# The first stage and the attention heads of a diffusion-transformer step, written out by hand for four queues

## Chip, cores and metric

The kernel runs as one program on one core of a Trainium2 chip. The metric is the time of one execution on the device in microseconds (us). The matmul engine TensorE is called PE in the profile, VectorE is DVE, ScalarE is ACT, GpSimd is POOL, and SyncE, whose queue issues nearly all DMAs here, is SP.

## The reference

Two streams of 256 tokens with 1024 features (the image tokens `x` and the context `ctx`) pass two layers. Each layer is: a SwiGLU feed-forward, a mixer, a second feed-forward; each part is preceded by an RMS norm that is modulated by a shift and a scale, and added back through a gate. Shift, scale and gate are columns of `silu(c) @ mod_w[i] + mod_b[i]`, one set for each stream. The mixer of layer 0 is a gated short convolution, that of layer 1 is attention with 8 query heads of 128 features and 2 key/value heads, whose keys are both streams (512) and whose queries are the image tokens (256).

```
for i in range(2):
    mod  = (silu(c) @ mod_w[i] + mod_b[i]).reshape(3, 3, D)        # shift, scale, gate, three times
    modc = (silu(c_ctx) @ mod_w[i] + mod_b[i]).reshape(3, 3, D)
    lat = lat + 0.5 * mod[0, 2] * swiglu(rms(lat) * g * (1 + mod[0, 1]) + mod[0, 0], w13, w2)   # and ctx
    lat = lat + mod[1, 2] * mixer(...)                              # conv, then attention
    lat = lat + 0.5 * mod[2, 2] * swiglu(..., w13', w2')
# attention, for each head: p = softmax(q k^T / sqrt(128)), p v, then @ w_o
```

Everything is float32. Layer 1 needs the context for its keys and values alone, so its last feed-forward runs on the image tokens only.

## The kernel before

**Layout.** Activations lie features on partitions, tokens along the free axis: `x` is 8 tiles of 128 features by 512 tokens (256 of each stream). A float32 product is made of three matmuls in a rounded format (`mm3`, lines 124 to 126 of the profile): each operand is split into a rounded high part and the rest (`split`: ACT copies to the high part, line 100, DVE subtracts, line 101), and the products high-high, high-low and low-high are summed in PSUM. So every weight that comes from memory into a `wr` tile (three of them, 1 MB each, `load_raw`, line 96, on SP) passes through ACT and DVE before PE can use it (`wh`, `wl`, four 1024-wide pairs). `hop` is a pool of sixteen 1024-wide operand tiles (`hot`), PSUM has six 512-wide tiles in one ring (`psum`) and two in another (`psmall`).

**Modulation.** The first two groups of modulation columns, shift B00 and scale A00 of the first norm, are made by PE in the first stage (`mod_pe`, steps P: eight small matmuls; `mod_turn`, steps T, turns the rows into columns; DVE adds the bias). All others are made on DVE, beside PE's work: a unit (`mod_unit`, line 154, `junk`) is a 1024-wide product and sum against the broadcast `silu(c)`, and a weight load of 1 MB in a `wr` tile serves two to four units. `tick(n)` puts n units at a place of the program.

**Order.** A scheduler orders each engine's instructions by its own estimates and priorities, except in the first stage, where PE's order alone is written out by hand (`FIRST_STEPS` inside `manual_schedule`). There, N is a quarter of the norm (DVE makes t = x*A*r, ACT hh = t + B, DVE hl), H the float32 copy of it that later sums need, W a block's weight load with its splits, M a quarter of a block's products, F fillers that keep PE busy, S the broadcast of `silu(c)`. The first three of 22 blocks of the first feed-forward are made in this stage: 144 matmuls of 512 columns. Behind it come `h.sums()`, the sums and splits of the norm's output that later blocks use (a Strassen-like scheme, class `Pair`), and `tick(4)`.

**DMA order.** SP's loads, and the ten small constants that ACT's queue loads (`cload`), take completion semaphores in turn from eight; a DMA waits until the one eight places ahead of it has landed, whichever queue that was issued from.

**Attention.** `scores(hd)` makes, for each of two query tiles, the 128 x 512 scores on PE (`psc`), their maximum (`mx`) and `nb` on DVE, the exponential `e` with its sum on ACT, the reciprocal `r` on DVE and the normalized `pn` on POOL. `turn` transposes `pn` on PE (`pt`) and splits it (`pth`, `ptl`); `mix` multiplies by the values on PE (`pav`) and splits the result (`a`). The program names them head by head, two heads ahead, and the scheduler orders all engines. The output projection (`py`) follows; its weights `wo` are four loads, split whenever the scheduler places it.

**Last feed-forward.** Image tokens only; the first four blocks run on operands that don't yet need the norm's sum (`Early`), the rest on both halves side by side (`mm_wide`, lines 132 and 134). Three modulation loads of the last gate fall into it and use `wr` tiles.

Of the kernel before, what the change touches and what calls it, by code (L numbers as in the profile page):

```python
# [16 lines left out]
P = 128  # L17
# [13 lines left out]
WARM = 36  # L31
FILL = 8
# [5 lines left out]
    "P10 P00 T10 T00 N0 F W0 M00 W1 P11 P01 T11 T01 N1 H0 M10 W2 M01 P12 H1 M11 P02 T12 T02 "  # L38
    "N2 M20 H2 M21 P13 P03 T13 T03 N3 M02 M12 M22 H3 M03 M13 M23 S"
# [4 lines left out]
def hybrid_kernel(ctx: ExitStack, tc: tile.TileContext, a: dict, out: bass.AP):  # L44
# [40 lines left out]

    sccol = const.tile([P, KT, 32], F32, name="sccol", tag="sccol")
# [12 lines left out]
    def split(hi, lo, src):  # L99
        nc.scalar.activation(out=hi, in_=src, func=AF.Copy)  # L100
        nc.vector.tensor_tensor(out=lo, in0=src, in1=hi.bitcast(F32), op=ALU.subtract)  # L101
# [45 lines left out]

    def mod_unit(l, ch, pair, raw, j, v):
# [5 lines left out]
        nc.vector.tensor_tensor_reduce(  # L154
            out=junk,
            in0=raw[:, j * D : j * D + D],
            in1=scbc[:, v, :],
            scale=1.0,
            scalar=modb[:, l, col : col + 1],
            op0=ALU.mult,  # L160
            op1=ALU.add,
            accum_out=mt[:, kt, v : v + 1],
        )
        done[l, ch] += 1
# [4 lines left out]
    def mod_job(l, ch, pair):  # L169
        mod_tile(l, ch)  # L170
        raw = load_raw(a["modT"][l, ch * 4 + pair])
# [9 lines left out]
    def next_unit():  # L181
        if not units:
            l, ch, pair = jobs.pop(0)
            mod_tile(l, ch)
            raw = load_raw(a["modT"][l, ch * 4 + pair])
# [544 lines left out]
    def ffn(l, b, h, tot, gate, tail, gs=(), ev=1.5, z=None):  # L730
        gs = list(gs)
        i0 = 0
        for t, n in enumerate(THIRDS):
            between = ()
            if tot == T2:
# [22 lines left out]
                for i in range(len(gs), n):  # L758
                    if t == 0 and not heads and i in AS_IS[l, b]:
                        w = load_w(a["w13"][l, b, i])  # L760
                        pp = psum("pg"), psum("pu")
                        if prev:
                            prev.seven()
                        w13_mm(pp, w, h, range(4), 0, T2)
# [109 lines left out]

    def mod_pe(ch, q):


        raws = []
        for i in range(2):
            raws.append(hot("pm", F32))  # L880
            nc.sync.dma_start(raws[i], a["mod0"][ch, q, :, i * 1024 : i * 1024 + 1024])
# [28 lines left out]
    def norm_q(q):  # L910
        k2 = slice(2 * q, 2 * q + 2)
        nc.vector.tensor_tensor(
            out=A00[:, k2, :], in0=A00[:, k2, :], in1=both(normg[:, 0, 0, k2]), op=ALU.mult
        )
        for k in range(2 * q, 2 * q + 2):
            for s in range(2):
                t = None
                if k % 2:
                    t = tp.tile([P, T2], F32, name=nm("t"), tag="sg", bufs=3)[:, :S]
                ts[k, s] = norm_k(s, k, h, A00, B00, ris[s], t)  # L920

    def copy_q(q):
        for s in range(2):
            h32[q, s] = gp.tile([P, T2], F32, name=nm("hr"), tag="gl" if s else "gh")
            for k in range(2 * q, 2 * q + 2):
                nc.scalar.activation(
                    out=h32[q, s][:, (k % 2) * S : (k % 2) * S + S], in_=ts[k, s],
                    func=AF.Identity, bias=B00[:, k, s : s + 1],
                )

    pps = {}
    ris, ts = [], {}

    def first_mm(i, q):
        if q == 0:
            pps[i] = psum("pg"), psum("pu")
        w13_mm(pps[i], ws[i], h, range(2 * q, 2 * q + 2), 0, T2)

    ws, gs0 = {}, []

    def load_sc():
        for v in range(2):
            nc.sync.dma_start(scbc[:, v, :], a["c2"][v : v + 1, :].to_broadcast([P, D]))
            nc.scalar.activation(out=scbc[:, v, :], in_=scbc[:, v, :], func=AF.Silu)

    def first_w(i):
        if i < 2:
            ws[i] = load_w(a["w13"][0, 0, i], fine=True)
            return
        raw = load_raw(a["w13"][0, 0, i])  # L950
        parts = [new_pair("w") for _ in range(4)]
        for j in (0, 2, 1, 3):
            split(*parts[j], raw[:, j * T2 : j * T2 + T2])
        ws[i] = lambda o: tuple(t[:, o % T2 : o % T2 + P] for t in parts[o // T2])
# [5 lines left out]
        "H": copy_q,  # L960
        "S": load_sc,
        "W": first_w,
        "N": norm_q,
        "M": first_mm,
    }
    with tc.manual_schedule(engines={mybir.EngineType.PE}):
        fill(WARM)
        sums = [rms_sum(s, (accs[s], accs[s, "last"])) for s in range(2)]
        for step in FIRST_STEPS.split():
            if step == "P00":  # L970
                for s in range(2):
                    ris.append(tp.tile([P, S], F32, name=nm("ris"), tag=f"ris{s}", bufs=1))
                    nc.scalar.copy(ris[s], rms_all(*sums[s]))
# [6 lines left out]
    h.sums()  # L980
    tick(4)

    convk = cload("convk", [P, 3, KT])
    qg = cload("qg", [P, 1])
    kg = cload("kg", [P, 1])
    cosT = cload("cosT", [P, S])
    sinT = cload("sinT", [P, S])
# [3 lines left out]
    ffn(0, 0, h, T2, lazy_gate(0, 0), tail_norm(0, 1, hn), gs0, 1.8)  # L991
# [42 lines left out]
    def by_pairs(key):  # L1034
        box = {}
# [21 lines left out]
    ffn(1, 0, h, T2, lazy_gate(1, 0), tail_norm(1, 1, hn), (), 1.4)  # L1057
# [134 lines left out]
    def scores(hd):  # L1192
        kv = hd // (HEADS // KVH)
        r_ = []
        for qt in range(2):
            o = (hd % 2) * S + qt * P
            ps = psum("psc")
            mm3(ps, tuple(t[:, o : o + P] for t in qs[hd // 2]), ks[kv], True, True)
            ci = hd * 2 + qt
            mx = ap.tile([P, 1], F32, name=nm("mx"), tag="mx", bufs=4)  # L1200
            nc.vector.reduce_max(mx, ps, axis=AX.X)
            nb = ap.tile([P, 1], F32, name=nm("nb"), tag="nb", bufs=4)
# [4 lines left out]
            e = tp.tile([P, T2], F32, name=nm("e"), tag="sg", bufs=3)  # L1207
            sm = ap.tile([P, 1], F32, name=nm("sm"), tag="smx", bufs=4)
            nc.scalar.activation(
                out=e, in_=ps, func=AF.Exp, scale=scq[:, ci : ci + 1], bias=nb, accum_out=sm  # L1210
            )
            r = ap.tile([P, 1], F32, name=nm("r"), tag="r", bufs=4)
            nc.vector.reciprocal(r, sm)
            if qt == 0:
                pn2 = hot("pn", F32)
            pn = pn2[:, qt * T2 : qt * T2 + T2]
            nc.gpsimd.tensor_scalar(out=pn, in0=e, scalar1=r, scalar2=None, op0=ALU.mult)
            r_.append(pn)
        return r_

    def turn(pn):
        pth, ptl = (hot(t).rearrange("p (b q) -> p b q", q=S) for t in ("pth", "ptl"))
        for qt in range(2):
            pt = psum("pt")
            for kt in range(4):
                nc.tensor.transpose(
                    pt[:, kt * P : kt * P + P], pn[qt][:, kt * P : kt * P + P], ident
                )
            split(
                pth[:, :, qt * P : qt * P + P], ptl[:, :, qt * P : qt * P + P],  # L1230
                pt.rearrange("p (k q) -> p k q", k=4),
            )
        return pth, ptl

    aos, at = [], []

    def mix(hd, pt):
        kv = hd // (HEADS // KVH)
        if hd % 2 == 0:
            t = hot("a")  # L1240
            at.append((t[:, :T2], t[:, T2:]))
        po = psum("pav")
        for kt in range(4):
            vw = tuple(t[:, kv * P : kv * P + P] for t in vs[kt])
            mm3(po[:, :S], vw, (pt[0][:, kt, :], pt[1][:, kt, :]), kt == 0, kt == 3)
        o = (hd % 2) * S
        ah, al = (t[:, o : o + S] for t in at[-1])
        split(ah, al, po[:, :S])
        aos.append((ah, al))

    pns, pts = {0: scores(0)}, {}
    v_proj(2)
    v_proj(3)
    tick(2)
    pns[1] = scores(1)
# [10 lines left out]
    project(  # L1266
        by_pairs("wo"), lambda k, c0, c1: aos[k], KT, lazy_gate(1, 1), tail_early(1, 2, hn, hz), S, 0, 0,
# [85 lines left out]
```

## Time and profile before

| | us |
|---|---|
| median of 3 runs (lowest, highest) | 1580.02 (1578.83, 1580.3) |
| the profiled execution | 1575.39 |
| its span on the core | 1573.6 |
| mean granted TensorE clock | 0.998 |
| PE busy | 1556.6 (99%) |
| DVE busy | 1330.8 (85%) |
| ACT busy | 735.2 (47%) |
| DMA, mean over the span | 158 GB/s |

The profiled execution's own time is 1.8 us above its span. Starts are counted from the start of the span. A matmul's duration is modelled and longer than its place in the pipeline: two wide matmuls that follow each other start about 0.23 us apart, though each is listed with 0.39. In brackets behind an instruction stands the idle time of its engine ahead of it and what ended that.

### The profile page before, as it was taken

The page shows a single profiled execution, that of the slowest core. Times are in us where ns is not written, and L with a number is a line of the kernel's source. Part 1 is how long each engine was busy: PE and PEld are TensorE (multiplying, and loading weights), DVE is VectorE, ACT ScalarE, POOL GpSimd, SP SyncE. Part 2 cuts the span into 40 slices and gives each one's busy share as a digit, 9 for nine tenths or more (in the row PEclk, how much of TensorE's full clock was granted, in tenths as well). Part 3 has the DMA queues.
Part 4 walks back from the last instruction along what each step waited for, and adds up shares of the span by engine and source line. Part 5 has one row for each costly group of instructions (what it writes and reads, how often), then busy time and mean ns, then how long its engine had stood idle before and what let it go on. Part 6 is the DMA issues. An engine that isn't in the chain of part 4 may idle for free.

```text
span 1573.6 us, 25030 instructions
## 1 busy us (share of the span) xinstructions
PE 1556.6 (99%) x10224; PEld 1421.7 (90%) x10224; DVE 1330.8 (85%) x2065; ACT 735.2 (47%) x1164; POOL 26.1 (2%) x20
## 2 busy tenths in 40 slices
PE   9999999999999999999999999999999999999999
PEld 7788998999888899989999899999899898898888
DVE  5989789979988779898798899788798889797676
ACT  6522452544322355435345375335345355665553
POOL 0000000000000000000000000000000003300000
PEclk9999999999999999999999999999999999999999
DMA  9565245334554422452353423442453555256552
GB/s 363 201 223 184 90 146 179 114 128 155 185 200 175 161 68 101 159 184 86 129 176 110 167 84 113 158 158 101 155 187 125 212 180 174 80 201 229 177 208 97
DMA packets 39571, 248.74 MB, mean 158 GB/s; under 512 B 5408, under 2 KB 7200, under 8 KB 14624
## 3 DMA queue, kind: packets, MB, share of 16 engines
q1 hardware_dynamic: 36864, 245.38, 43.8%
q10 hardware_dynamic: 2592, 1.76, 0.4%
q8 instruction: 80, 1.31, 0.3%
q14 instruction: 35, 0.29, 0.1%
HBM read 244.77 MB, written 1.05 MB: 156 GB/s over the span
## 4 chain that ended last, share of the span: by engine, by line
PE 93%; DVE 3%; ACT 2%; DMA 2%; issue 0%; ACTq 0%; DVEq 0%
PE py L125 9%; PE py L126 9%; PE py L124 9%; PE p L126 7%; PE p L125 7%; PE p L124 7%; PE q L124 5%; PE q L126 5%; PE q L125 5%; PE py L132 2%; PE pg L132 2%; PE pu L132 2%; PE pu L126 1%; PE pg L124 1%; PE pu L125 1%; PE pu L124 1%
## 5 line engine op out<-in xcount | busy, mean ns | idle before, releaser
L100 ACT ACTIVATE wh<-wr 128x1024 fp32r<-128x1024 f32 (+2 forms) x276 | 276.4, 1014 | 350.0 <-PE py L125 107.1
L101 DVE TENSOR_TENSOR wl<-wr,wh 128x1024 fp32r<-128x1024 f32 (+2 forms) x276 | 320.7, 1168 | 57.1 <-ACT wh L100 56.8
L154 DVE CUSTOM_DVE_ANT_0 junk<-wr,scbc,modb 128x1024 bf16<-128x1024 f32 x224 | 287.2, 1282 | 32.5 <-DMA wr<-in_modT 30.0
L124 PE MATMUL py<-gh,wh 128*128 128x512 f32 (+1 forms) x570 | 213.3, 374 | 0.0
L125 PE MATMUL py<-gl,wh 128*128 128x512 f32 (+1 forms) x570 | 213.2, 374 | 0.0
L126 PE MATMUL py<-gh,wl 128*128 128x512 f32 (+1 forms) x570 | 213.0, 374 | 0.0
L101 DVE TENSOR_TENSOR wl<-ws,wh 128x1024 fp32r<-128x1024 f32 x108 | 131.8, 1223 | 26.2 <-ACT wh L100 25.9
L100 ACT ACTIVATE wh<-ws 128x1024 fp32r<-128x1024 f32 x108 | 113.7, 1058 | 80.2 <-PE p L125 32.8
L126 PEld LDWEIGHTS py<-gh,wl 128*128 128x128 f32 x570 | 107.3, 188 | 19.0
L124 PEld LDWEIGHTS py<-gh,wh 128*128 128x128 f32 x570 | 107.4, 188 | 18.6
L125 PEld LDWEIGHTS py<-gl,wh 128*128 128x128 f32 x570 | 107.4, 188 | 18.2
L126 PE MATMUL p<-th,wl 128*128 128x256 f32 x432 | 122.3, 283 | 0.0
L125 PE MATMUL p<-tl,wh 128*128 128x256 f32 x432 | 122.2, 283 | 0.0
L124 PE MATMUL p<-th,wh 128*128 128x256 f32 x432 | 122.2, 283 | 0.0
L534 DVE SCALAR_TENSOR_TENSOR x<-py,G,x 128x256 f32<-128x256 f32 x189 | 83.9, 479 | 25.1 <-PE py L126 12.1
L124 PE MATMUL q<-bh,wh 128*128 128x256 f32 x320 | 90.6, 283 | 0.0
L125 PE MATMUL q<-bl,wh 128*128 128x256 f32 x320 | 90.6, 283 | 0.0
L126 PE MATMUL q<-bh,wl 128*128 128x256 f32 x320 | 90.6, 283 | 0.0
L124 PEld LDWEIGHTS p<-th,wh 128*128 128x128 f32 x432 | 82.9, 192 | 0.3
L125 PEld LDWEIGHTS p<-tl,wh 128*128 128x128 f32 x432 | 82.9, 192 | 0.3
L126 PEld LDWEIGHTS p<-th,wl 128*128 128x128 f32 x432 | 82.9, 192 | 0.0
L676 DVE TENSOR_TENSOR ws<-wr 128x1024 f32<-128x1024 f32 x54 | 65.8, 1219 | 0.7 <-DMA wr<-in_w 0.7
(288 smaller groups left out, 4019.3 us busy)
## 6 DMA issues: line engine op xcount, KB each, us to landing
wr<-in_w SPq DMA_DIRECT2D x88, 1024.0 KB, 4.9
wr<-in_modT SPq DMA_DIRECT2D x64, 1024.0 KB, 4.9
wr<-in_w2b SPq DMA_DIRECT2D x32, 896.0 KB, 4.6
wr<-in_w2a SPq DMA_DIRECT2D x16, 1024.0 KB, 4.8
pm<-in_mod SPq DMA_DIRECT2D x16, 512.0 KB, 9.2
wr<-in_cw_cx SPq DMA_DIRECT2D x8, 1024.0 KB, 4.9
wr<-in_cw_b SPq DMA_DIRECT2D x4, 1024.0 KB, 5.8
wr<-in_cw_out SPq DMA_DIRECT2D x4, 1024.0 KB, 4.9
```

The source lines that it names most:

```text
L100: nc.scalar.activation(out=hi, in_=src, func=AF.Copy)
L101: nc.vector.tensor_tensor(out=lo, in0=src, in1=hi.bitcast(F32), op=ALU.subtract)
L124: nc.tensor.matmul(ps, wh, mh, start=first, stop=False, **kw)
L125: nc.tensor.matmul(ps, wh, ml, start=False, stop=False, **kw)
L126: nc.tensor.matmul(ps, wl, mh, start=False, stop=last, **kw)
L132: nc.tensor.matmul(ps, w[0], m[2], start=first and n == 0, stop=False)
L154: nc.vector.tensor_tensor_reduce(out=junk, in0=raw[:, j * D : j * D + D], in1=scbc[:, v, :], scale=1.0, scalar=modb[:, l, col : col + 1], ...
L534: nc.vector.scalar_tensor_tensor(out=x[:, m, s * S : s * S + S], in0=ps[:, o : o + S], scalar=g[:, m, s : s + 1], in1=x[:, m, s * S : s * ...
L676: tt(out=sm.rearrange("p (a b c) -> p a b c", a=2, b=2)[:, :, 0, :], in0=a21.unsqueeze(1).to_broadcast([P, 2, T2]), in1=self.raw[:, T2 : 3 ...
```

## The change

- **First stage, all four queues.** The order of PE, DVE, ACT and SP is written out. Loads are steps of their own (L a modulation load; R half of a block's weights, two 512-wide quarters, 0.5 MB), W splits a single quarter, X makes the inverse norms, U makes x*g*r ahead of the modulation, N does one 128-feature tile (ACT hh from A and B, the float32 copy in place on DVE or ACT, DVE hl). The first products of blocks 0 and 1 are named by part: h is high-high, w uses the low part of the weights, l that of the activations. Fillers: 32 and 5 instead of 36 and 8. A Silu on a constant stands ahead of the first real one. The constants for the convolution and the attention are issued behind the stage's last Silu; `h.sums()` moves into block 3's code, `tick(4)` is gone, and two feed-forwards have larger ticks.
- **Attention.** The order of PE, DVE, ACT and POOL is written out over all heads, with the last two `v_proj` between the first two heads. The first two loads of `wo` come ahead of the heads, and each is split in four quarters, one in each of loop steps 2 to 5 and two in each of the last two; where there is a head to run ahead, the quarter stands ahead of its second exponential. The `tick(2)` between the heads is gone.
- **Last feed-forward.** From the output projection on, a modulation load goes as two halves into operand tiles of `hop` and no longer into a `wr` tile.

```diff
-WARM = 36
-FILL = 8
+WARM = 32
+FILL = 5
 FIRST_STEPS = (
-    "P10 P00 T10 T00 N0 F W0 M00 W1 P11 P01 T11 T01 N1 H0 M10 W2 M01 P12 H1 M11 P02 T12 T02 "
-    "N2 M20 H2 M21 P13 P03 T13 T03 N3 M02 M12 M22 H3 M03 M13 M23 S"
+    "L10 L00 R00 R10 P10 X U0 L11 P00 L01 T10 T00 W00 N00 W01 N01 F h000 w000 l000 R20 W10 "
+    "W11 h001 w001 h100 h101 l001 l100 l101 U1 P11 L12 P01 L02 T11 T01 w100 w101 N10 N11 W20 "
+    "W21 U2 M01 R01 R11 P12 L13 P02 L03 T12 T02 M11 R21 N20 N21 W02 W03 M20 W12 W13 U3 M21 "
+    "P13 P03 T13 T03 W22 W23 M02 N30 N31 M12 M22 M03 M13 M23 S"
 )
...
+    def load_mod(l, ch, pair):
+        src = a["modT"][l, ch * 4 + pair]
+        if not roomy:
+            raw = load_raw(src)
+            return raw[:, :D], raw[:, D:]
+        raw = hot("wm", F32), hot("wm", F32)
+        for j in range(2):
+            nc.sync.dma_start(raw[j], src[:, j * D : j * D + D])
+        return raw
...
+    def scale_q(q):
...
+                nc.vector.scalar_tensor_tensor(
+                    out=raw_of(k, s), in0=x[:, k, s * S : s * S + S],
+                    scalar=normg[:, 0, 0, k : k + 1], in1=ris[s], op0=ALU.mult, op1=ALU.mult,
+                )
+    def norm_one(q, j):
...
+            nc.scalar.activation(
+                out=hs[s][0], in_=raw_of(k, s), func=AF.Identity, scale=ab[s][0], bias=ab[s][1]
+            )
...
+            if q == 0 or j == 0:
+                nc.vector.tensor_scalar(
+                    out=r, in0=r, scalar1=ab[s][0], scalar2=ab[s][1], op0=ALU.mult, op1=ALU.add
+                )
+            else:
+                nc.scalar.activation(out=r, in_=r, func=AF.Identity, scale=ab[s][0], bias=ab[s][1])
...
+    def first_raw(i, hf):
+        if hf == 0:
+            raws[i] = wp.tile([P, 2048], F32, name=nm("wr"), tag="wr", bufs=3)
+        part = lambda t: t.rearrange("p (a b c) -> p a b c", a=2, b=2)[:, :, hf, :]
+        nc.sync.dma_start(part(raws[i]), part(a["w13"][0, 0, i]))
...
-    with tc.manual_schedule(engines={mybir.EngineType.PE}):
+    queues = [nc.tensor, nc.vector, nc.scalar, nc.sync]
+    with tc.manual_schedule(engines={e.engine for e in queues}):
...
-    h.sums()
-    tick(4)
-    convk = cload("convk", [P, 3, KT])
+    with tc.issue_after(rows["last"]):
+        convk = cload("convk", [P, 3, KT])     # and qg, kg, cosT, sinT
-    ffn(0, 0, h, T2, lazy_gate(0, 0), tail_norm(0, 1, hn), gs0, 1.8)
+    ffn(0, 0, h, T2, lazy_gate(0, 0), tail_norm(0, 1, hn), gs0, 2)
-    ffn(1, 0, h, T2, lazy_gate(1, 0), tail_norm(1, 1, hn), (), 1.4)
+    ffn(1, 0, h, T2, lazy_gate(1, 0), tail_norm(1, 1, hn), (), 1.5)
...
-    for hd in range(HEADS):
-        if hd + 2 < HEADS:
-            pns[hd + 2] = scores(hd + 2)
-        pts[hd] = turn(pns.pop(hd))
-        if hd:
-            mix(hd - 1, pts.pop(hd - 1))
-    mix(HEADS - 1, pts.pop(HEADS - 1))
+    with tc.manual_schedule(engines={e.engine for e in (nc.tensor, nc.vector, nc.scalar, nc.gpsimd)}):
+        for hd in range(2):
+            for qt in range(2):
+                heads[hd].scores(qt)
+                heads[hd].top(qt)
+                heads[hd].exp(qt)
+            for qt in range(2):
+                heads[hd].share(qt)
+            v_proj(2 + hd)
+        for i, hd in enumerate(heads):
+            ahead = heads[i + 2] if i + 2 < HEADS else None
+            for qt in range(2):
+                if ahead:
+                    ahead.scores(qt)
+                    ahead.top(qt)
+                hd.turn(qt)
+                if ahead and qt:
+                    ahead.share(0)
+                hd.turned(qt)
+                if not ahead or qt and 2 <= i < 6:
+                    split(*pieces.pop(0))
+                if ahead:
+                    ahead.exp(qt)
+            if ahead:
+                ahead.share(1)
+            if i:
+                heads[i - 1].mix()
+        heads[-1].mix()
...
+    roomy.append(True)
     project(
```

In the new attention code `scores` is the three matmuls of a query tile, `top` mx and nb, `exp` the exponential, `share` the reciprocal and POOL's product, `turn` the transposes, `turned` their split, `pieces` the quarters of `wo`.

More of the change, by code (lines that the diff above doesn't have):

```diff
@@ L84, in hybrid_kernel @@
     nc.vector.memset(eps_t, EPS)
+    nc.scalar.activation(
+        out=const.tile([P, 1], F32, name="silu", tag="silu"), in_=eps_t, func=AF.Silu
+    )
     sccol = const.tile([P, KT, 32], F32, name="sccol", tag="sccol")
@@ L763, in ffn @@
                             prev.seven()
+                        if "T1" not in h.t:
+                            with tc.issue_after(rows["W1"]):
+                                h.sums()
                         w13_mm(pp, w, h, range(4), 0, T2)
@@ L873, in hybrid_kernel, with mod_load @@
     rows = {}
+    def mod_load(ch, q):
+        rows[ch, q] = [hot("pm", F32) for _ in range(2)]
+        for i in range(2):
+            nc.sync.dma_start(rows[ch, q][i], a["mod0"][ch, q, :, i * 1024 : i * 1024 + 1024])
     def mod_pe(ch, q):
[L878 to L881, printed above, removed]
+        raws = rows[ch, q]
         pr = psum("pr") if (ch, q) == (1, 0) else psmall("pr")
@@ L908, in mod_turn, with first_inv, raw_of @@
         )
[L910 to L914, printed above, removed]
+    def first_inv():
+        for s in range(2):
+            ris.append(tp.tile([P, S], F32, name=nm("ris"), tag=f"ris{s}", bufs=1))
+            nc.scalar.copy(ris[s], rms_all(*sums[s]))
+    def raw_of(k, s):
+        return h32[k // 2, s][:, (k % 2) * S : (k % 2) * S + S]
+    def scale_q(q):
+        for s in range(2):
+            h32[q, s] = gp.tile([P, T2], F32, name=nm("hr"), tag="gl" if s else "gh")
@@ L934, in first_mm, with first_part, part @@
+    def first_part(lo):
+        def part(i, q, j):
+            if (q, j, lo) == (0, 0, 0):
+                pps[i] = psum("pg"), psum("pu")
+            k = 2 * q + j
+            for n in range(2):
+                nc.tensor.matmul(
+                    pps[i][n], ws[i]((1 - n) * 1024 + k * P)[lo == 2],
+                    pick(h, k, 0, T2)[lo == 1],
+                    start=(k, lo) == (0, 0), stop=(k, lo) == (KT - 1, 1),
+                )
+        return part
     def first_mm(i, q):
-        if q == 0:
-            pps[i] = psum("pg"), psum("pu")
@@ L1211, in scores, with share @@
             )
+        def share(self, qt):
             r = ap.tile([P, 1], F32, name=nm("r"), tag="r", bufs=4)
-            nc.vector.reciprocal(r, sm)
+            nc.vector.reciprocal(r, self.sm[qt])
             if qt == 0:
[L1215 to L1224, printed above, removed]
-            for kt in range(4):
[L1226 to L1249, printed above, removed]
@@ new lines, in turn, with turned @@
+        def turn(self, qt):
+            if qt == 0:
+                self.hi, self.lo = (
+                    hot(t).rearrange("p (b q) -> p b q", q=S) for t in ("pth", "ptl")
+                )
+            pt = self.pt[qt] = psum("pt")
+            for kt in range(4):
+                o = qt * T2 + kt * P
+                nc.tensor.transpose(pt[:, kt * P : kt * P + P], self.pn[:, o : o + P], ident)
+        def turned(self, qt):
+            src = self.pt[qt].rearrange("p (k q) -> p k q", k=4)
+            split(*(t[:, :, qt * P : qt * P + P] for t in (self.hi, self.lo)), src)
@@ new lines, in mix @@
+        def mix(self):
+            po = psum("pav")
+            for kt in range(4):
+                vw = tuple(t[:, self.kv * P : self.kv * P + P] for t in vs[kt])
+                mm3(po[:, :S], vw, (self.hi[:, kt, :], self.lo[:, kt, :]), kt == 0, kt == 3)
+            if self.hd % 2 == 0:
+                t = hot("a")
+                at.append((t[:, :T2], t[:, T2:]))
+            o = (self.hd % 2) * S
+            aos.append(tuple(t[:, o : o + S] for t in at[-1]))
+            split(*aos[-1], po[:, :S])
```

139 lines of the change are left out of this document (83 added, 56 removed).

## The prediction

> **What bounds the kernel now.** I read the page first, then busy time by stage, then TensorE's order of time in the stages with idle time, and there the queues that end its waits. From the page the busy line; from the view by stretches (stretch, length, then busy us and instructions of PE, PEld, DVE, ACT, POOL, then granted clock, DMA share, GB/s) the four stages:
>
> ```profile
> PE 1556.6 (99%) x10224; PEld 1421.7 (90%) x10224; DVE 1330.8 (85%) x2065; ACT 735.2 (47%) x1164; POOL 26.1 (2%) x20
> ...
> 0.00:66.90 66.90, 63.74 (x416) 49.99 (x417) 46.84 (x107) 43.76 (x85) 0.19 (x4) 0.97 0.75 290
> 66.90:1308.00 1241.10, 1238.12 (x8157) 1141.57 (x8156) 1083.77 (x1595) 547.11 (x812) 0.00 (x0) 1.00 0.42 149
> 1308.00:1358.00 50.00, 44.70 (x311) 39.23 (x311) 43.01 (x106) 33.19 (x78) 25.94 (x16) 1.00 0.36 122
> 1358.00:1573.60 215.60, 210.06 (x1345) 190.86 (x1343) 157.17 (x259) 111.16 (x191) 0.00 (x0) 1.00 0.50 176
> ```
>
> TensorE bounds the program. In the 1241 us of the middle it idles 3.0 us: nothing is to be had there, only lost. The change works in the first 67 us (idle 3.2 us, and filler matmuls that count as busy), in attention (5.3 us idle in 50) and in the last feed-forward (5.5 us idle in 216). So its whole field is some 15 to 20 us, 1% of the time.
>
> **First stage.** The order of time on PE (start, duration, line, operation, count):
>
> ```profile
> 15.32 0.64 PE L886 MATMUL pr<-pm,sccol 128*32 128x256 f32 x8
> 17.03 0.64 PE L886 MATMUL pr<-pm,sccol 128*32 128x256 f32 x8 [1.07 <-DMA pm<-in_mod]
> 17.60 1.21 PE L898 MATMUL pr<-rowsum,row 128*128 128x2 f32 x8
> 18.67 3.66 PE L859 MATMUL idle<-ones 128*128 128x128 f32 x16
> 22.16 0.49 PE L124 MATMUL pg<-hh,wh 128*128 128x512 f32 x1
> ...
> 47.41 2.06 PE L886 MATMUL pr<-pm,sccol 128*32 128x256 f32 x32
> ...
> 50.48 0.48 PE L124 MATMUL pg<-hh,wh 128*128 128x512 f32 x1
> ...
> 66.68 0.39 PE L126 MATMUL pu<-hh,wl 128*128 128x512 f32 x1
> ```
>
> From 50.48 to 66.68 lie 71 steps of 0.228 us, with nothing between them, so the stage's last matmul gives way at 66.91. A late set of P and T steps takes 50.48 - 47.41 = 3.07 us. The stage's 144 wide matmuls and three such sets are 144 x 0.228 + 3 x 3.07 = 42.0 us of work; they took 66.91 - 22.16 = 44.75. So 2.7 us are lost behind the first wide matmul, and the rest ahead of it.
>
> Ahead of it three things move. First, the data. The traffic (columns here: clock, DMA share, GB/s), a wait of the DMA queue's own engine (total, times, longest), and what held ACT:
>
> ```profile
> 10.00:12.00 2.00, 1.00 0.99 339
> 12.00:14.00 2.00, 1.00 0.49 170
> 14.00:16.00 2.00, 1.00 1.01 395
> ...
> SPq L96 <- DMA qg<-in_qg: 4.7, 1, 4.7
> ...
> 10.68 0.68 ACTq L70 DMA_DIRECT2D cosT<-in_cosT  x1
> 11.39 1.28 ACT L254 ACT_TABLE_LOAD   x1 [0.46 <-issue]
> ```
>
> A weight load waited 4.7 us for `qg`, a small constant of ACT's queue, to land; from 10 to 14 us the DMA fell (56 + 225) x 2 = 562 KB short of 395 GB/s, 1.4 us of transfer. The change issues those five constants behind the stage, so the second half of P00 should land that much sooner. PE can use it only behind the first half, which ran at 15.32: 17.03 - 15.32 - 0.57 (17.03 to 17.60 is a half) leaves 1.1 us, and 0.45 more where ACT's table load, and the rms products behind it, no longer stand behind the issue of `cosT`. Bounds 0 and 1.55 us; I take 1.3, near the upper end, since both causes are rows. Second, eight fillers lasted from 18.67 to 22.16, 0.436 us each; five are 1.3 us less (bounds: 0 where the operands are late, and 1.3). Third, the operands: the product x*g*r is made ahead of T00 (step U), and then hh needs A and B alone.
>
> ```profile
> 19.17 0.15 DVE L903 TENSOR_TENSOR mod<-pr,modb 128x4 f32<-128x4 f32 x1
> 19.36 1.31 ACT L286 ACTIVATE hh<-t,mod 128x256 fp32r<-128x256 f32 x3 [1.21 <-DVE mod L903]
> 21.62 1.29 DVE L101 TENSOR_TENSOR wl<-wr,wh 128x512 fp32r<-128x512 f32 x2
> L1015 DVE TENSOR_SCALAR d<-u,convk 128x512 f32<-128x512 f32 x8 | 3.9, 483 | 0.0
> ```
>
> T would start at 16.3, the fillers end at 16.3 + 1.07 + 5 x 0.436 = 19.55. B is there at 17.6, two hh (0.43 each) at 18.6: in time. DVE then has a weight quarter (0.64), two rescalings, two 256-wide subtractions (about half a quarter, 0.34 each) and the second quarter. The 256-wide rescaling is not in the trace: between 0.24 (half of L1015's 483 ns) and 0.48. At 0.4 the second quarter is ready at 20.4 and needed at 19.55 + 3 x 0.228 = 20.2: 0.2 us lost. Further down the written order P11 follows ten pairs of partial products, at about 24 us; its data lies 2.1 MB behind P00's, 5.3 us at 395 GB/s, and has landed, so the waits of before are gone. The second quarter's hh and hl cost some 0.3, and the first matmul behind each P set 0.1. That is 0.8 where 2.7 were lost (bounds 0.3 and 2.7). First stage: 1.3 + 1.3 + 1.9 = 4.5 us.
>
> What is pushed out of the stage: `h.sums` (eight 512-wide splits and six sums), whose splits the scheduler now sets among block 3's, and four modulation units. Block 3's second weight half must come from DVE 24 x 0.228 + 0.5 = 6 us behind M03; ahead of it stand four 512-wide operations and a 1024-wide one, some 4 us. Block 4's halves come behind 14 us of such work and have 6 + 48 x 0.228 = 17. The cover is DVE's idle time, 20 us in the first stage and 157 in the middle; were it gone, four units and the sums at 0.64 an operation would cost 5 us and more. The larger ticks replace units taken out elsewhere, under the same cover: nothing. The early Silu table load, the weight loads by halves and the later constants are off the path behind the start: nothing.
>
> **Attention.** First PE, then DVE and ACT:
>
> ```profile
> 1321.09 0.40 PE L124 MATMUL psc<-kh,qh 128*128 128x512 f32 x1
> ...
> 1325.29 0.47 PE L124 MATMUL psc<-kh,qh 128*128 128x512 f32 x1
> ...
> 1344.44 0.39 PE L124 MATMUL pav<-pth,vh 128*128 128x256 f32 x1
> ...
> 1345.96 0.40 PE L124 MATMUL psc<-kh,qh 128*128 128x512 f32 x1
> ...
> 1347.36 0.60 PE L1226 MATMUL pt<-ident,pn 128*128 128x128 f32 x4
> ...
> 1350.40 1.04 PE L1226 MATMUL pt<-ident,pn 128*128 128x128 f32 x8
> ...
> 1357.78 0.28 PE L125 MATMUL py<-a,wh 128*128 128x256 f32 x1
> ...
> 1344.75 0.68 DVE L1201 TENSOR_REDUCE mx<-psc 128x1 f32<-128x512 f32 x1
> 1345.47 0.21 DVE L1203 TENSOR_SCALAR nb<-mx,scq 128x1 f32<-128x1 f32 x1
> ...
> 1345.78 0.78 ACT L1209 ACTIVATE e<-psc,nb,scq 128x512 f32<-128x512 f32 x1
> 1346.55 1.08 ACT L100 ACTIVATE pth<-pt 128x512 fp32r<-128x512 f32 x2
> 1347.51 0.39 ACT L100 ACTIVATE a<-pav 128x256 fp32r<-128x256 f32 x1
> ```
>
> From the scores of head 1 (1321.09) to the projection alone (1357.78) are 36.7 us. The change writes a head's order out: on DVE mx, nb, ptl, mx, nb, r, ptl, (wl), r, a; on ACT pth, e, pth, (wh), e, a, the quarter of the output weights in heads 2 to 5 of the loop. From the rows: mx to nb 0.72, nb to e 0.31, e 0.77, pth 0.48; ptl 0.64, a quarter on ACT 0.51 (as 512-wide as pth, a little longer), a 0.38. With mx at 0, e starts at 1.03 and ends at 1.80, pth at 2.28, the quarter at 2.79, the second e at 3.56, a at 3.94, and DVE's a (0.34) at 4.3. Without the quarter the second e waits for its nb, 0.72 + 0.12 + 0.60 + 0.72 + 0.31 = 2.47, and the head ends at 4.0. PE needs 1.40 for two scores, 0.8 for two turns and 1.5 for the mix, 3.7: DVE and ACT set the pace. Six heads: 3.4 (no mix yet) + 4.0 + 4 x 4.3 = 24.6. The last two: on DVE four operations and an a, 2.7, then three more, 1.8, and the last mix, 1.5: 6.0. With 0.9 from a first score to its mx and head 1's two scores ahead, 1.4, that is 32.9: 3.8 us less, of which I keep 3.6. Behind a waiting e stand the next pth and a; behind a waiting r stand ptl, a and the next mx, and PE's score waits for none of these until its PSUM tile is short. Bounds: PE's 3.7 would gain 2.4 more; the pace of before, (1350.40 - 1325.29) / 5 = 5.0 with weight splits between, would cost 5.5, so a loss of 1.9. Nearest is a late head without weights, 1350.40 - 1345.96 = 4.44.
>
> **Last stage.** A wait of SP, then SP, ACT and PE in order of time:
>
> ```profile
> SPq L96 <- DVE mod L154: 0.8, 1, 0.8
> ...
> 1409.37 3.27 SPq L96 DMA_DIRECT2D wr<-in_w  x2
> ...
> 1416.61 1.06 ACT L100 ACTIVATE wh<-wr 128x1024 fp32r<-128x1024 f32 x1 [1.27 <-DMA wr<-in_w]
> ...
> 1418.94 1.42 PE L132 MATMUL pg<-hx,wh 128*128 128x512 f32 x5 [2.17 <-ACT wh L100]
> ```
>
> A block's weights were issued only when DVE's modulation unit had freed a `wr` tile; ACT had them 7.2 us later, and PE stood 2.17 us. With the modulation weights in operand tiles, `wr` holds weights alone. On SP the six half loads may wait for an operand tile with weight loads behind them, but those tiles come free with the projection, blocks earlier. Bounds 0 and 2.17; I take 2.1, as the wait named is the one removed.
>
> **Sum.** 4.5 + 3.6 + 2.1 = 10.2 us. The profiled execution took 1575.39 us, 1.8 more than its span, and would take 1565.2; the median of the runs, 1580.02, is 4.6 above it, and becomes 1569.8.
>
> **Rivals.** (a) *The clock eats the start.*
>
> ```profile
> 18.80:22.10 3.30, 3.30 (x17) 3.26 (x16) 3.30 (x9) 2.74 (x7) 0.00 (x0) 0.50 1.00 415
> ```
>
> For 3.3 us PE was granted half the clock, and only fillers suffered. If that stretch comes again at the same hour, the wide matmuls from 19.55 to 22.1 are hit: 1.3 us lost, 1571.1. Against it: PE's idle microsecond ahead of it should go. [...] (b) *Attention gains nothing*: a pace of 5.0 a head, 10.2 - 5.5 = 4.7 us, 1575.3. For it: the lists couple DVE and ACT four times a head. (c) *Slower: the head loop closes.* If a score had to wait for its PSUM tile until the head before is done, nothing would overlap, and a head would cost 2 x (0.9 + 0.72 + 0.31 + 0.77) + 1.5 = 6.9 us, 16.8 more over six heads: 1586.6. It decides from some 6.3 a head. For it: six PSUM tiles serve five allocations a head. Against: the tile that a score takes was last read a head earlier. (d) *The stalls only move*: the pushed-out DVE work returns as waits of 5 us in the middle, and the last stage's wait stays: 1577, and with more of it no change at all.
>
> **Chances.** Forecast 0.6, (a) 0.14, (b) 0.15, (c) 0.05, (d) 0.06. A measurement of this kernel can tell about 0.2%, 3.2 us, from no change. Faster takes the first three, 0.89; same most of (d), 0.05; slower (c) and a little, 0.06. The forecast alone runs from 1566.5 (heads at PE's pace and a little more) to 1573; with (a), (b) and the bounds of the stage, 1566.5 to 1576.
>
> **What would show it.** Right: the first wide matmul at 19 to 20 us, the third block of the first stage done near 62.4; heads 4.0 to 4.4 us apart; no wait for wh in the last feed-forward. Wrong: the half clock under pg and pu at the start; heads 5 us apart, with DVE waiting for e and e for nb in turn; new waits of PE for wh, wl or tl from 62 us on.

## The result, and the profile after

| | median us (lowest to highest, runs) | the profiled execution: time, span, clock |
|---|---|---|
| before | 1580.3 (1578.83 to 1581.44, 5) | 1575.39, 1573.6, 0.998 |
| after | 1572.11 (1571.1 to 1573.51, 5) | 1573.51, 1571.7, 0.998 |

The ratio is 0.995, with an interval of 0.9936 to 0.9965: 8.2 us faster, where 10.2 were forecast. But the two traces differ by 1.9 us of span, not by 8.2. So the first question is where the medians come from, and the second where the forecast's 10.2 us are in the trace.

The page's busy line, and the view by stretches with cuts at the same places of the program as in the prediction's four stages (block 3, the kri transposes ahead of the heads, the first output projection):

```profile
PE 1556.1 (99%) x10210; PEld 1420.0 (90%) x10210; DVE 1334.4 (85%) x2075; ACT 731.4 (47%) x1159; POOL 25.0 (2%) x20
```

```profile
0.00:64.90 64.90, 61.19 (x402) 47.85 (x403) 45.17 (x105) 39.10 (x72) 0.19 (x4) 0.97 0.81 299
64.90:1309.20 1244.30, 1238.24 (x8135) 1140.23 (x8134) 1087.56 (x1603) 546.88 (x814) 0.00 (x0) 1.00 0.42 149
1309.20:1356.10 46.90, 45.03 (x319) 39.59 (x318) 42.44 (x99) 33.15 (x74) 24.85 (x16) 1.00 0.28 96
1356.10:1571.70 215.60, 211.65 (x1359) 192.38 (x1357) 159.28 (x271) 112.25 (x201) 0.00 (x0) 1.00 0.52 181
```

The same stretches of before:

```profile
66.90:1305.50 1238.60, 1235.62 (x8135) 1139.07 (x8134) 1081.27 (x1591) 545.94 (x810) 0.00 (x0) 1.00 0.42 149
1305.50:1356.30 50.80, 45.50 (x319) 40.03 (x319) 44.50 (x101) 33.23 (x70) 25.94 (x16) 1.00 0.39 130
1356.30:1573.60 217.30, 211.76 (x1359) 192.56 (x1358) 158.18 (x269) 112.30 (x200) 0.00 (x0) 1.00 0.50 175
```

The first stage is 2.0 us shorter, attention 3.9, the end 1.7; and the middle, with as many matmuls (x8135), is 5.7 us longer, its idle time (length less PE's busy time) 6.1 instead of 3.0. Two rows of PE in order of time show a part of that idle time, and VectorE's order at the same place shows why:

```profile
601.77 0.38 PE L132 MATMUL q<-th,wh 128*128 128x256 f32 x1 [0.55 <-ACT wh L108]
603.03 0.38 PE L134 MATMUL q<-th,wl 128*128 128x256 f32 x1 [0.52 <-DVE wl L109]
```

```profile
598.74 1.28 DVE L175 CUSTOM_DVE_ANT_0 junk<-wr,scbc,modb 128x1024 bf16<-128x1024 f32 x1
599.94 0.08 DVE L175 DVE_READ_ACCUMULATOR2_ANT mod<- 128x1 f32 x1
599.94 0.68 DVE L703 TENSOR_TENSOR ws<-wr,ws 128x512 f32<-128x512 f32 x1
600.54 1.28 DVE L175 CUSTOM_DVE_ANT_0 junk<-wr,scbc,modb 128x1024 bf16<-128x1024 f32 x1
601.75 0.08 DVE L175 DVE_READ_ACCUMULATOR2_ANT mod<- 128x1 f32 x1
601.75 1.23 DVE L109 TENSOR_TENSOR wl<-ws,wh 128x1024 fp32r<-128x1024 f32 x1
```

Two modulation units (`junk`, 1.28 us each) stand within one pair of blocks; the weights' sums (`ws`) and `wl` behind the second one come late, and PE waits. At 1166 us it is the same: units at 1161.71 and 1163.52, and PE waits 0.76 us for `wl`. VectorE has nothing to spare at such a place: from 594 to 604 us it is busy for 9.92 of 10 us.

In the start, the order of time on PE of this execution, and of a second profiled execution of the same kernel:

```profile
14.50 1.87 PE L285 MATMUL ss<-ident,ri 128*128 128x128 f32 x8
16.31 1.94 PE L912 MATMUL pr<-pm,sccol 128*32 128x256 f32 x16
18.17 1.21 PE L924 MATMUL pr<-rowsum,row 128*128 128x2 f32 x8
20.83 0.50 PE L986 MATMUL pg<-hh,wh 128*128 128x512 f32 x1 [0.23 <-ACT hh L959]
64.93 0.39 PE L132 MATMUL pg<-hh,wh 128*128 128x512 f32 x1
```

```profile
14.16 1.16 PE L285 MATMUL ss<-ident,ri 128*128 128x128 f32 x8
15.33 1.07 PE L912 MATMUL pr<-pm,sccol 128*32 128x256 f32 x16
16.33 1.21 PE L924 MATMUL pr<-rowsum,row 128*128 128x2 f32 x8
17.40 1.36 PE L883 MATMUL idle<-ones 128*128 128x128 f32 x10
18.99 0.50 PE L986 MATMUL pg<-hh,wh 128*128 128x512 f32 x1 [0.23 <-ACT hh L959]
19.85 0.39 PE L986 MATMUL pg<-hh,wl 128*128 128x512 f32 x1
20.71 0.50 PE L986 MATMUL pu<-hh,wl 128*128 128x512 f32 x1 [0.46 <-DVE wl L109]
63.09 0.39 PE L132 MATMUL pg<-hh,wh 128*128 128x512 f32 x1
```

The same 16 matmuls of P00 took 1.94 us in one execution and 1.07 in the other. The granted clock (third number from the end) tells them apart, first execution first:

```profile
14.80:18.10 3.30, 3.30 (x24) 1.88 (x22) 1.76 (x4) 1.00 (x3) 0.00 (x0) 0.50 1.07 408
```

```profile
14.80:18.10 3.30, 3.29 (x35) 2.42 (x34) 2.27 (x7) 1.90 (x5) 0.00 (x0) 1.00 1.07 408
```

### The profile page after: what moved, and what is told of

The parts are those of the page before. It is cut to its first block, busy times and chain, and to the rows that moved or that the text cites. A ratio compares the mean times of both kernels' runs of the same rounds, so it can differ in the third digit from the quotient of the medians.

```text
span 1571.7 us, 24988 instructions
## 1 busy us (share of the span) xinstructions
PE 1556.1 (99%) x10210; PEld 1420.0 (90%) x10210; DVE 1334.4 (85%) x2075; ACT 731.4 (47%) x1159; POOL 25.0 (2%) x20
## 3 DMA queue, kind: packets, MB, share of 16 engines
HBM read 244.77 MB, written 1.05 MB: 156 GB/s over the span
## 4 chain that ended last, share of the span: by engine, by line
PE 88%; DVE 5%; ACT 3%; DMA 3%; issue 1%; POOL 0%; POOLq 0%; ACTq 0%; DVEq 0%; SPq 0%
PE py L132 8%; PE py L133 8%; PE py L134 8%; PE p L132 6%; PE p L134 6%; PE p L133 6%; PE q L134 5%; PE q L132 5%; PE q L133 5%; PE py L140 2%; PE pu L140 2%; PE pg L140 2%; DVE wl L109 1%; DMA wr<-in_modT 1%; PE py L142 1%; PE pu L134 1%
## 5 line engine op out<-in xcount | busy, mean ns | idle before, releaser
L175 DVE CUSTOM_DVE_ANT_0 junk<-wr,scbc,modb 128x1024 bf16<-128x1024 f32 x218 | 279.3, 1281 | 30.4 <-DMA wr<-in_modT 27.6
```

What stands on the lines that cost most here:

```text
L175: nc.vector.tensor_tensor_reduce(out=junk, in0=raw[j], in1=scbc[:, v, :], scale=1.0, scalar=modb[:, l, col : col + 1], op0=ALU.mult, op1=A ...
```

## The experiments

**What an execution is made of.** The experiments and the executions of after give 159 timed executions of 12 kernels, each with span and granted clock; the kernel before has two rows, and its five executions of the table above are not among them, as their clock is not on record. The line span = c + s x 1000 x (1 - clock), with one s for all and a c for each row, leaves 1.05 us (standard deviation; 3.3 at most): s is 1.21 us (standard error 0.06) for each .001 of clock. A stretch of 3.4 us at half clock (18.76 to 22.17 us in before) is 1.7/1573 = .0011 of mean clock, so by this line it costs 1.3 us. The column c is what a kernel would take at full clock, by the same line; "at full clock" below means a difference of two c:

| kernel | executions | median us | mean clock | c, us of span (error) |
|---|---|---|---|---|
| before | 60 | 1579.2 | .9960 | 1572.5 (0.3) |
| before again | 12 | 1579.45 | .9958 | 1572.9 (0.4) |
| before + first stage and ticks | 12 | 1579.25 | .9965 | 1573.0 (0.4) |
| before + last modulation weights | 11 | 1579.51 | .9956 | 1572.2 (0.4) |
| before + heads | 6 | 1574.03 | .9972 | 1568.9 (0.5) |
| after (both times) | 10 | 1572.3 | .9977 | 1568.0 (0.4) |
| after, 36 warming matmuls | 5 | 1571.15 | .9982 | 1567.7 (0.5) |
| after, quarter behind the exponential | 9 | 1573.64 | .9981 | 1570.0 (0.4) |
| after, last weights in `wr` | 12 | 1574.68 | .9974 | 1570.4 (0.3) |
| after, units as before | 5 | 1568.33 | .9974 | 1563.0 (0.5) |
| after, 1.8 and 1.4 units alone | 6 | 1566.37 | .9982 | 1562.7 (0.4) |
| after, units as before, 36 warming | 5 | 1566.86 | .9980 | 1562.9 (0.5) |
| the last, ScalarE held up | 6 | 1568.65 | .9980 | 1564.4 (0.5) |

**Before again**, no edit.

> The kernel before, unchanged, for a second profile and for the spread of its executions. Question: the traces of before and after differ by 1.9 us of span, the medians by 8.2, and in the traces the middle (block 3 of the first stage to the kri transposes) is 5.6 us longer after the change. Theory 1 (the change costs nothing in the middle; the one profiled execution of before was a short one): this second profile's middle is longer than 1238.6 us, by up to 5 us. Theory 2 (the middle's loss comes from the change): the middle is 1238.6 us again, and what before's median has over its profiled execution lies elsewhere, most likely in the first stage. Time against before: same, within 0.1%.

Ratio 1.0003 (0.9992 to 1.0014). Its profiled execution had the middle 4.1 us longer than the first one of before, with three half-clock stretches there instead of one, and two more in the heads:

```profile
1330.90:1334.20 3.30, 1.88 (x12) 1.00 (x10) 3.30 (x7) 3.27 (x9) 2.93 (x3) 1.00 0.26 30
1334.30:1337.60 3.30, 2.23 (x7) 1.74 (x7) 3.30 (x7) 2.43 (x5) 3.30 (x3) 0.50 0.71 288
1337.70:1341.00 3.30, 3.30 (x14) 2.90 (x14) 1.91 (x6) 0.38 (x1) 2.64 (x2) 0.50 0.79 263
```

Here a stretch with 1.4 us of idle PE is followed by two at half clock. The first profiled execution had few of them: its mean clock was .9978, that of all 60 is .9960, and the difference is 2.3 us by the line. So half of the 4.6 us between that execution and its median are half-clock stretches; 0.8 is the median of three executions against that of 60 (1580.02 and 1579.2), and 1.5 is scatter about the line. Theory 1 is right about before; it does not clear the change, as the next run shows.

**Before with the first stage's part**: all of the change but the `Head` section and `roomy`.

> Before with the first stage's part alone: its new order on four queues, constants late, five fillers, the six sums set in block 3, the larger ticks. Prediction: 4.5 us faster than before, the middle not longer. By the two traces: the stage gains 2.0 us; if the pushed-out DVE work costs the 5.6 us in the middle, this kernel is 1 to 4 us slower than before.

Ratio 1.0003 (0.9991 to 1.0014): no gain at all, though block 3 starts at 64.72 us. The prediction's 4.5 us fail here, and the loss of 1 to 4 us that the traces suggested doesn't come either (0.5 at full clock, error 0.3). From the first residual update to the kri transposes it took 1179.4 us, with two half-clock stretches in them; before + heads took 1175.0 with two, before 1173.7 with one.

**Before with the heads' part**: the `Head` section, without the `tick(2)` that stood between the heads, and the loads of `wo` alone.

> Before with the attention heads' part alone (written order, weight quarters in the loop). Prediction: 3.6 us faster than before. By the traces: 3.9 us, from the kri transposes to the first projection. Rival (no gain in the heads, or one that is lost later): within 1 us of before.

Ratio 0.9969 (0.9958 to 0.998). At full clock 3.6 us are gained, the prediction's number; the median gains 1.5 more, as the clock rises from .9960 to .9972 in six executions. PE's listed idle time in the heads is 1.8 us instead of 5.3, and no half-clock stretch lies in them.

**Before with the last modulation weights in operand tiles**: `load_mod` and `roomy.append(True)` alone.

> Before with the last modulation weights in operand tiles alone. Prediction: 2.1 us faster, and no wait for wh in the last feed-forward. By the traces: 1.4 us, because a wait for wl of 0.8 us stays in its place. Rival (the wait only moves): 0 to 0.5 us.

Ratio 1.0005 (0.9994 to 1.0016): the rival. The wait is still there, 2.04 us for `wh` at 1405.06, and a half-clock stretch behind it.

**After again**, and **after with 36 warming matmuls**.

```diff
-WARM = 32
+WARM = 36
```

> The changed kernel again, for a second profile and more executions. Theory (the gain is of two kinds): at equal granted clock it is about 4.5 us ahead of before, and its executions hold fewer half-clock stretches than before's (mean clock .9978 against .9961), which is the rest of the 7 to 8 us. Rival (the clock differences of the first executions were chance): its mean clock is .996 as before's, and the gain shrinks to 4.5 us.

> The changed kernel with 36 warming matmuls as before the change, not 32. Theory: with 32 TensorE stands 1.5 us ahead of the sums of squares (row of after: ss at 11.63, 1.54 idle), and that idle time brings the half-clock stretch at 14 to 18 us onto P00 and T; with 36 the idle time is gone, T starts 0.5 to 1 us sooner (near 17.3) and the kernel is 0.5 to 1.5 us faster than the changed one. Rival: the stretch comes from the narrow matmuls of the sums, whatever the warming: T stays at 17.9 to 18.2, and the time is the same within 0.3 us.

After again: 0.9963 (0.995 to 0.9975); at full clock 4.6 us ahead of before, mean clock .9977 against .9960, so 2.1 us more. So the theory of two kinds of gain holds. With 36: no idle time ahead of the sums, T at 16.92 (with 32 it was 18.17 and 16.33), 0.3 us at full clock, within the error. Neither execution had a half-clock stretch between 13 and 18 us. Of all seven profiles of the new first stage with 32 three had it, of the three with 36 none: too few to say whether 32 bring it more often.

**After with the modulation units as before.**

```diff
+    tick(4)
-    ffn(0, 0, ..., gs0, 2)
+    ffn(0, 0, ..., gs0, 1.8)
-    ffn(1, 0, ..., (), 1.5)
+    ffn(1, 0, ..., (), 1.4)
```

> The changed kernel with the modulation units placed as before: four units behind the first stage, 1.8 and 1.4 a block. Theory: the waits for wh and wl near 601 us (0.55 and 0.52) and near 1166 us (0.76) come from two units set where before had one; they go, the middle is 1 to 3 us shorter and the kernel faster by as much, unless the four units stall block 3 (new waits for wl at 65 to 80 us, up to 3 us). Rival: the waits come from elsewhere (the six sums, transfers): they stay, and the time is the same within 0.5 us.

1568.33 us: 4.1 under the changed kernel that ran beside it, 4.9 at full clock. The waits at 601 and 1166 us are gone, and block 3 has none, though the four units stand behind the first stage again.

**After with 1.8 and 1.4 alone**, without the `tick(4)`.

> The changed kernel with 1.8 and 1.4 units a block as before, but still without the four units behind the first stage. Theory 1 (the larger ticks set two units where before had one): it is as fast as the kernel with all units placed as before, 1568.3 us, 4 us under the changed one. Theory 2 (the four units left out early are what is missing, and they are caught up where VectorE has little idle time): no gain, 1572 us, or slower still, since the units then fall due in one heap.

1566.37 us, 0.9916 of before (0.9899 to 0.9932): at full clock as fast as the previous run, so it is the larger ticks, theory 1. The units in the stretches from the first residual update on (columns: VectorE busy with units and their count, clock, DMA share, GB/s), after and then this kernel, with two neighbouring units of this kernel behind them; the first stretch is the rest of the first feed-forward, the second holds the waits at 601 us, the third is that part of layer 1's first feed-forward which matches the first, and the fourth leads from there to the kri transposes:

```profile
129.70:358.00 228.30, 49.98 (x39) 1.00 0.40 143
358.00:669.10 311.10, 83.25 (x65) 0.99 0.42 150
...
1019.70:1240.30 220.60, 38.28 (x30) 1.00 0.43 151
1240.30:1309.20 68.90, 10.79 (x10) 1.00 0.55 191
```

```profile
127.70:355.20 227.50, 44.83 (x35) 1.00 0.39 139
355.20:663.70 308.50, 83.29 (x65) 1.00 0.43 151
...
1014.20:1232.90 218.70, 34.59 (x27) 1.00 0.41 142
1232.90:1301.60 68.70, 13.21 (x11) 1.00 0.55 195
```

```profile
594.39 1.28 DVE L175 CUSTOM_DVE_ANT_0 junk<-wr,scbc,modb 128x1024 bf16<-128x1024 f32 x1
...
601.07 1.28 DVE L175 CUSTOM_DVE_ANT_0 junk<-wr,scbc,modb 128x1024 bf16<-128x1024 f32 x1
```

The larger ticks put 39 and 30 units where 35 and 27 had been, at a loss of 0.8 and 1.9 us. The count alone does not tell the loss: around 601 us both kernels have 65 units, and after is 2.6 us longer there. The units that run ahead shift the later ones: in after two fall into one pair of blocks (598.74 and 600.54), while here 6.7 us lie between two. From start to start the two matmuls that wait there lose 1.4 us; the rest of the 2.6 is a half-clock stretch, which this execution has elsewhere (.99 and 1.00). Without the larger ticks the middle is that of before again, in length and in idle time (3.0 us). It has 207 units where after has 213; the six stand behind the heads, four of them at the output projection, 1352.14 to 1357.76 us (12 units from 1348.3 us on, 6 behind the heads in after), and PE doesn't wait for `wl` there:

```profile
62.90:1301.60 1238.70, 1235.73 (x8135) 1139.33 (x8134) 1081.23 (x1591) 549.07 (x814) 0.00 (x0) 1.00 0.42 147
```

This version beats both kernels; the run with all units as before can't be told from it.

**After with the quarter behind the exponential.**

```diff
-                if not ahead or qt and 2 <= i < 6:
-                    split(*pieces.pop(0))
                 if ahead:
                     ahead.exp(qt)
+                if not ahead or qt and 2 <= i < 6:
+                    split(*pieces.pop(0))
```

> The changed kernel with a head's weight quarter split behind its second exponential. By the prediction's list the quarter on DVE then ends 0.5 us later and holds r and a behind it: 4.8 us a head against 4.3, 2 us slower over four heads. Rival (DVE and ACT do not set the pace): the same time within 0.5 us; or, if the exponential set it, 1 us faster.

2.1 us slower at full clock. The first maximum of a loop step on VectorE, after (steps 1 to 4) and then this kernel (steps 3 and 4, and the quarter ahead of step 3):

```profile
1331.22 0.67 DVE L1278 TENSOR_REDUCE mx<-psc 128x1 f32<-128x512 f32 x1
...
1335.19 0.68 DVE L1278 TENSOR_REDUCE mx<-psc 128x1 f32<-128x512 f32 x1
...
1339.51 0.68 DVE L1278 TENSOR_REDUCE mx<-psc 128x1 f32<-128x512 f32 x1
...
1343.82 0.68 DVE L1278 TENSOR_REDUCE mx<-psc 128x1 f32<-128x512 f32 x1
```

```profile
1337.19 0.68 DVE L1278 TENSOR_REDUCE mx<-psc 128x1 f32<-128x512 f32 x1
...
1342.09 0.68 DVE L1278 TENSOR_REDUCE mx<-psc 128x1 f32<-128x512 f32 x1
```

```profile
1336.19 0.69 DVE L109 TENSOR_TENSOR wl<-wr,wh 128x512 fp32r<-128x512 f32 x1 [0.79 <-ACT wh L108]
1336.80 0.16 DVE L1296 RECIPROCAL r<-sm 128x1 f32<-128x1 f32 x1
1336.87 0.41 DVE L109 TENSOR_TENSOR a<-pav,a 128x256 fp32r<-128x256 f32 x1
```

In after a step takes 4.0 us without a quarter and 4.3 with one; here a step with a quarter takes 4.9, as VectorE stands 0.79 us for the quarter, with r and a behind it.

**After with the last modulation weights in `wr` again**: without `roomy.append(True)`.

> The changed kernel with the last modulation weights in wr tiles again. Prediction: 2.1 us slower than the changed kernel, with the wait for wh near 1410 to 1420 us back. By the traces with the new heads (68.5 to 69.8 us from the attention projection's residual to the next against 67.1): 1.4 to 2.8 us slower. Rival (the stage is held by VectorE, the wait only moves, as in before with this part alone): within 0.5 us.

2.5 us slower at full clock, so in the changed kernel this part is worth its 2.1 us. The row of its longest wait, and the stretch of clock behind it; then the one wait that after has left there:

```profile
1398.49 0.58 PE L134 MATMUL pu<-zh,wl 128*128 128x258 f32 x1 [2.20 <-DVE wl L109]
```

```profile
1394.90:1398.30 3.40, 1.39 (x12) 1.18 (x10) 3.40 (x8) 2.81 (x7) 0.00 (x0) 1.00 0.23 94
1398.40:1401.70 3.30, 3.21 (x15) 3.21 (x16) 3.30 (x7) 0.81 (x2) 0.00 (x0) 0.50 0.31 45
```

```profile
1419.34 1.21 PE L142 MATMUL pg<-hx,wl 128*128 128x256 f32 x8 [0.79 <-DVE wl L109]
```

With the units as before that wait is gone too, and the stage takes 214.8 us instead of 215.6. Why the part is worth 2.5 us here and 0.4 in before is settled only in part: with the new heads and without it PE waits twice, 2.2 and 1.2 us (before + heads, a last stage of 218.6 us), where before waits once, 2.17 us (217.2). Why the wait stays in before with this part is open.

**Units as before and 36 warming matmuls**, and **the same with ScalarE held up in one head**.

```diff
+                if (i, qt) == (3, 0):
+                    hole = ap.tile([P, 2, T2], BF16, name="hole", tag="hole", bufs=1)
+                    for _ in range(2):
+                        nc.scalar.activation(out=hole, in_=x[:, :2, :], func=AF.Copy)
```

(As run, two copies, not the three that the expectation names.)

> The changed kernel with the modulation units placed as before and 36 warming matmuls: 1568.3 us less the 0.8 us for which TensorE still stood ahead of the sums, of which about half is real work pulled forward: 1567.5 to 1568.3 us. Rival (36 matmuls only fill that wait): 1568.3.

> The last kernel (units as before, 36 warming matmuls) with three 1024-wide copies on ScalarE into an unused tile in the fourth head, some 3.1 us of ScalarE's time that nobody needs; the result is untouched. Theory (idle time of TensorE costs a second time, by the granted clock): TensorE stands 2 to 3 us in that head, a half-clock stretch of 3.41 us follows in most executions, and the kernel is 3.5 to 4.5 us slower, its mean granted clock lower by .0005 to .001. Rival (idle time costs itself alone): 2 to 3 us slower, the same mean clock.

1566.86 us: the warming matmuls add nothing that can be told from none. The held-up kernel is 1.5 us slower at full clock, at the same mean clock (.9980); PE stood 1.25 us, not 2 to 3, and no half-clock stretch followed. That agrees with the rival, but the hole was not the one that the theory names: that idle time brings the stretches is argued from what stood ahead of them in the traces, and no run shows it by an edit.

## Why the prediction was right, and where it was not

The time came out within the range, 2.3 us above the forecast, and part of that is luck. One step that was put at nothing cost 5.2 us, and the clock gave back 2.1 us that were not in the sum. The terms of the sum themselves came out at 9.8 us together. And the 8.2 us of the result are more than the 6.9 of all executions, because before stood at 1580.3 there and at 1579.2 in the 60 later ones.

- **First stage, 4.5 us: 3.8 in an execution without the half-clock stretch** (block 3 at 63.09 against 66.91), 2.0 in the first profile. T at 16.3 was right (16.33), so was the cause, the second half of P00 landing early: no wait for `pm` is left. The first wide matmul came at 18.99, not 19.55, as fillers at full clock last 0.27 us, not 0.436. The stalls behind it were mis-sized: 63.09 - 18.99 = 44.1 us for 42.0 of work, 2.1 lost instead of 0.8. A wait listed with 0.46 us costs 0.63: its matmul starts 0.86 us behind the one ahead of it (20.71 and 19.85), not 0.23.
- **Rival (a), half clock at the start**, came true at a price of 18.17 - 16.33 = 1.8 us, not 1.3. It hit P00 and T, not the wide matmuls, and other executions did without. The idle time named against it, 1.07 us of waiting for `pm`, did go, and the stretch came at 14.75 all the same.
- **The middle, nothing: the step that failed.** "The larger ticks replace units taken out elsewhere, under the same cover: nothing" cost 1568.0 - 1562.7 = 5.2 us. That is rival (d)'s 5 us by the price and not by the cause, which it saw in the work pushed out of the first stage. The cover, 157 us of VectorE's idle time in 1241, is a sum over the whole middle; where two units fall into one pair of blocks and the pair's sums are due, there is none (9.92 us busy of 10 around 601 us). What the prediction said of that pushed-out work held: `h.sums` costs nothing that shows, as the middle of the run with 1.8 and 1.4 is as long as that of before, and the four units cost nothing in either place (1562.7 us without the `tick(4)`, 1563.0 with it).
- **Attention, 3.6 us: 3.6** at full clock. The pace was the one forecast, 4.0 us a step without a quarter and 4.3 with one, and it is DVE's order that sets it, as the run with the quarter behind the exponential shows (4.9). Rivals (b) and (c) fell.
- **Last stage, 2.1 us: 2.5** in the changed kernel, 0.4 with this part alone, so the reason given (the wait named is the one removed) is too simple: in before the wait stays, and in after 0.79 us of waiting for `wl` is left, which goes with the larger ticks.
- **The sum, 10.2 us at the profile's clock**: at full clock 9.8 without the larger ticks, 4.6 with them. Less 3.6 for the heads and 2.5 for the last stage, the 9.8 leave 3.7 for the first stage, near the 3.8 of the trace.
- **From the profiled execution to the median.** The 4.6 us were carried over as a constant. Half of them were half-clock stretches, and the changed kernel has fewer: 1579.2 - 1572.3 = 6.9 us over all executions is 4.6 at full clock and 2.1 by the clock, within 0.2. That they go because PE's idle time goes, in the heads above all, is argued and not shown.

## What to carry to other kernels

Cover is local: before a helper's work is moved at no cost, count it stage by stage against that stage's idle time, not against the sum; and within a stage ask what else the helper owes at that place. Where the granted clock differs between executions (.992 to 1.000 for before), one profiled execution is one draw: compare kernels at equal granted clock, and read what the clock adds from the spread of all executions. Whether an idle wait of the bounding engine costs a second time, by the clock, was not shown here: half clock followed a wait of 2.20 us in one kernel (1398.49), and full clock one of 2.17 us in another (1418.94).

## What the runs showed of the hardware

- PE fell to half clock (0.50) for stretches of 3.41 us, at other places in other executions: at 18.76 and 568.31 us in before, at 14.75 and 567.71 in after. In the 3.4 us ahead of these four it stood 1.1, 0.8, 0.3 and 1.3 us. In three other traces, of the 3.3 or 3.4 us ahead of half clock it stood 1.4 (before again, at 1334.3), 2.1 (before + first stage, at 1406.9) and 2.0 (after with the last weights in `wr`, at 1398.4; the wait of 2.20 us in the row at 1398.49). The wait of 2.17 us in before (at 1418.94; 2.1 us of idle PE from 1415.5 to 1418.9) was followed by full clock, and so was the one of 1.25 us in the held-up kernel. So the amount of idle time alone does not tell where a stretch follows, and what does was not shown.
- One kernel's executions spread by 8 us (before, 1573.98 to 1581.95 in 30 that ran together), and the granted clock tells most of it: at .999 and 1.000 the spans were 1572.2 to 1573.8 us, at .994 they were 1579.0 to 1580.2. In before + heads the spread was 2 us (1573.27 to 1575.25), but in 6 executions only, and other kernels with the new heads spread by 6 and 7 us (1563.95 to 1569.97 in 6 with 1.8 and 1.4 units alone, 1572.37 to 1579.42 in 12 with the last weights in `wr`).
